# Covering a layer norm with matrix work: the order around it fixed, its chain put first, four more covering products; one pooled block moved ahead of the attention

## The chip, the cores and the metric

The kernel runs on one core of a Trainium2 chip. TensorE (PE in the profile) multiplies matrices out of SBUF into eight PSUM banks; VectorE (DVE) and ScalarE (ACT) do the elementwise work; SyncE (SP) issues the loads and stores, one after the other from one queue. The metric is the device time of one execution in microseconds (us), the median of several runs. Each engine works its own instructions in a fixed order and waits for the others through semaphores.

## The reference, cut to what matters

One step of a decoder layer on 16 meta, 512 prompt and 8 sample tokens, all in float32:

```python
z = h @ w_in + b_in                         # 2048 -> q 1024 | k 256 | v 256 | pool input u 1024
attn = sink_attention(rope(q), rope(k), v)  # window of 128, 16 heads, a learned sink for each
pool = (causal means of u over 2/4/8/16 - u) @ w_pool * pool_scale
h1 = layer_norm(alpha * h + concat(attn, pool) @ w_o)
a = silu(h1 @ w_gate) * (h1 @ w_up)         # 2048 -> 5632
y = layer_norm(alpha * h1 + a @ w_down)     # 5632 -> 2048
```

The 520 tokens that go past the mixer are worked in two halves of 260 columns (half 0 and half 1).

## The kernel before, in words

**A precise product.** A float32 weight is split into a high part (ACT, a CAST to `fp32r`, `split`, L181) and the remainder (DVE, L182), and so are the activations. A block of 128x128 weights then takes three passes on PE (`products`, L188, L189 and L191): high by high, high by low, low by high. A plain float32 matmul needs no split; the profile shows it as two records.

**The order.** The program is written once and an automatic scheduler sets each engine's order from a simulated timeline and from priorities. `with step(engine)` ties it down: what that engine does within the step comes after what it did in the step before.

**Attention.** `block("q0")` to `block("q7")` make the eight query blocks and `block("u0")` to `block("u7")` the eight pooled blocks: 96 matmuls each into two banks tagged `mm`, which DVE then empties. For each head pair t come the scores (`sc`, L525), the softmax on DVE and ACT, the turn of the probabilities (`tp`, L569 to L576) and the values (`o`, L587). Query and pooled blocks stand between, to cover the softmax and the copies. `pool_group(0)` to `pool_group(3)` (`pm`) are the small maps of the pooled blocks. `smT`, `smp`, `smpt`, `smo` are the sample tokens' attention.

**The two layer norms after the output projection.** `out_proj(h)` makes half h, and `ln1(h)` normalises it. `ln1` is a generator: each `yield` lets the caller put other work in. It takes the mean by a float32 matmul with a matrix of ones (L851, `mean`), subtracts it on DVE (L865), squares on ACT (L867), sums the squares by 16 float32 matmuls (L861, `var`), makes the reciprocal root (L221 to L227) and scales (DVE L879, ACT L882). The first layer norm runs beside `out_proj(1)`. The second has no such neighbour.

**Seven products in place of eight.** The gate and up projections use Winograd's form of Strassen's scheme: for each pair of weight tiles (a `Set`; `g0`, `u0`, `g1`, `u1`, ... up to 44) seven half-size products P1 to P7 of 24 matmuls. P1 needs the normalised half 0 alone (`b11`), P2 as well (`b21`); the other five need half 1, P3 to P6 through the operands `t1` to `t4` made from both halves (DVE L898 to L906, `put` L844 and L845), P7 through `t3`. DVE forms the weights' sums and differences (L927).

**The cover.** While the second layer norm runs, PE makes P1 of the first ten sets (`NFILL`, `Set.fill`, L951) from unsplit float32 operands, eight float32 matmuls each; ACT copies each result to SBUF (L953). No step holds this part: the scheduler chose where `mean`, `var` and the fills stand. Weight loads go through a ring of five buffers (`NRAW`); a fill's buffer comes free when its matmuls are done.

Of the kernel before, what the change touches and what calls it, by code (L numbers as in the profile page):

```python
# [13 lines left out]
P = 128  # L14
# [22 lines left out]
WPRIO = 400  # L37
NFILL = 10
NF = 5
LP = 600  # L40
WK = 7
WA = 4
# [21 lines left out]
def hybrid_step(ctx, tc, xin, w_in, w_o, w_g, w_u, w_d, w_pool, par_d, cst_d, ident_d, ln2gb, kct_d, vc_d, hist_d,  # L64
                ck_d, cv_d, sp_d, yp, ys, nkp, nvp, npp, nks, nvs, nps):
    nc = tc.nc
# [173 lines left out]
    with ExitStack() as sa:  # L240
# [183 lines left out]
        for h in range(2):  # L424
            for g in range(4):
                n = h * 4 + g + 1
# [316 lines left out]

        sample = sample_attention()
        block("q0")
        order = ["q1 q2", "q3 u0", "q4 u1", "q5 u2", "q6 u3", "q7 u4", "u5 u6", "u7"]
        for t in range(8):
            with step(pe):
                if t:
                    att_values(t - 1)  # L750
                sc = att_scores(t, qs.pop(t))
                if t >= 6:
                    next(sample)
            att_softmax(t, sc)
            done, us = us, []
            if t == 7:
                with step(pe):
                    for u in done:
                        next(u)
                    next(pool_group(2))  # L760
            for n, name in enumerate(order[t].split()):
                if n == 1:
                    with step(pe):
                        att_turn(t)
                        for u in done:
                            next(u)
                        if t == 6:
                            next(sample)
                    if t in (3, 5):
                        with step(pe):  # L770
                            next(pool_group((t - 3) // 2))
                block(name)
        with step(pe):
            att_turn(7)
# [72 lines left out]
    def ln1(h, zs):  # L847
# [15 lines left out]
        for k2 in range(8):  # L863
            a = z1[h][k2]
            nc.vector.tensor_sub(a, a, both(mean))  # L865
            sqs.append(t_tile(f"sq{h}_{k2}"))
            nc.scalar.activation(sqs[k2], a, AF.Square)  # L867
            if k2:
                var(k2 - 1)
            if k2 % 2:  # L870
                yield
        var(7)
        with tc.high_priority(LP):
# [38 lines left out]
    class Set:  # L912


        def __init__(self, w, i, name):
            self.w, self.i, self.name = w, i, name
            self.raw, self.p1 = {}, None

        def q(self, r, c):
            if (r, c) not in self.raw:  # L920
# [23 lines left out]
                    hi, lo = bop[b][k // 2]  # L944
                    products([bk], wh[:, sl], wl[:, sl], [hi[:, k % 2, :]], [lo[:, k % 2, :]], k == 0 and first, k == 7, True)

        def fill(self, t):

            bk = bank(f"p1_{self.name}")
            for k in range(8):  # L950
                nc.tensor.matmul(bk, self.q(0, 0)[:, k * P:(k + 1) * P], z1[0][k // 2][:, k % 2, :], start=(k == 0),  # L951
                                 stop=(k == 7))
            nc.scalar.copy(t, bk)  # L953
            self.p1 = t
            self.raw = {}

        def run(self, c11, c12, c21, c22):

            r = row_tile(f"p_{self.name}")
            filled = self.p1 is not None  # L960
            al, ga, de = [bank(f"{n}_{self.name}") for n in ("pa", "pc", "pd")]
            if not filled:
                self.p1 = r[:, HALF[0]]
                self.prod(1, al)
                nc.scalar.copy(self.p1, al)
            self.prod(7, ga)
# [234 lines left out]
```

## Time and profile before

| | |
|---|---|
| median of 3 runs | 2011.4 us (2010.8 to 2012.12) |
| the profiled execution's own time | 2010.83 us |
| its span, first to last instruction | 2009.0 us |
| PE busy | 1964.4 us, 98% of the span |
| DVE busy | 1341.8 us, 67% |
| ACT busy | 903.6 us, 45% |
| mean granted clock of PE | 0.988 |

"Busy" counts a matmul from its start to its modelled end, so PE counts as busy while matmuls come one after the other, at whatever speed they come. The granted clock says at what share of full speed PE was let run. A row of the timeline gives start, length, engine, line, output and input, and in square brackets how long the engine stood idle before it and what it waited for.

### The profile page before, as it was taken

What the parts mean: (1) busy time and instruction counts of PE and PEld (TensorE: products, weight loads), DVE (VectorE), ACT (ScalarE), POOL (GpSimd) and SP (SyncE); (2) the same over time, 40 slices, a digit from 0 to 9 for tenths busy, and PEclk for the clock granted to TensorE, in tenths of its full rate; (3) what the DMA queues carried; (4) which work ended last, traced back from release to release, by engine and by line L of the source; (5) the groups of instructions that cost most, each with busy time, mean ns of one, the idle gap of its engine ahead of it and who ended that gap; (6) DMA issues with size and microseconds to landing.
All of it is one profiled execution on the core that took longest, in us unless ns stands there. A gap on an engine that the chain in (4) does not pass through costs nothing.

```text
span 2009.0 us, 39879 instructions
## 1 busy us (share of the span) xinstructions
PE 1964.4 (98%) x16083; PEld 1936.3 (96%) x16083; DVE 1341.8 (67%) x2458; ACT 903.6 (45%) x1757; POOL 2.5 (0%) x8
## 2 busy tenths in 40 slices
PE   8999999999998999999999999999999999999996
PEld 8989999999978999999999999999999999999996
DVE  6666666766758888778777877787773433333586
ACT  6643445544554444544554455445552322222442
POOL 0000000000000000000000000000000000000000
PEclk9999999999998999999999999999999999999998
DMA  8622222665743444333333333333374633323554
GB/s 264 225 84 72 71 87 70 210 200 169 237 152 106 153 142 146 107 125 118 124 109 122 121 121 112 119 123 120 114 249 125 186 124 90 116 91 98 164 178 138
DMA packets 105625, 275.48 MB, mean 137 GB/s; under 512 B 12176, under 2 KB 35288, under 8 KB 105336
## 3 DMA queue, kind: packets, MB, share of 16 engines
q1 hardware_dynamic: 104320, 270.83, 42.2%
q8 instruction: 126, 2.06, 0.4%
q10 hardware_dynamic: 1120, 2.10, 0.3%
q14 instruction: 59, 0.48, 0.1%
HBM read 248.02 MB, written 27.41 MB: 137 GB/s over the span
## 4 chain that ended last, share of the span: by engine, by line
PE 94%; DVE 3%; DMA 1%; ACT 1%; issue 0%; SPq 0%; DVEq 0%; ACTq 0%
PE d L191 6%; PE d L189 6%; PE d L188 6%; PE pa_g L188 4%; PE pa_u L188 4%; PE pa_u L191 4%; PE pa_g L189 4%; PE pa_u L189 4%; PE pa_g L191 4%; PE o L188 3%; PE o L191 3%; PE o L189 3%; PE pc_g L188 2%; PE pc_u L188 2%; PE pc_g L189 2%; PE pc_u L191 2%
## 5 line engine op out<-in xcount | busy, mean ns | idle before, releaser
L181 ACT CAST rr<-fr 128x512 fp32r<-128x512 f32 (+1 forms) x1064 | 644.3, 612 | 918.4 <-PE d L189 245.1
L182 DVE TENSOR_TENSOR rr<-fr,rr 128x512 fp32r<-128x512 f32 (+1 forms) x1064 | 703.0, 677 | 414.7 <-ACT rr L181 401.0
L927 DVE TENSOR_TENSOR fr<-fr 128x1024 f32<-128x1024 f32 x176 | 215.3, 1223 | 64.0 <-DMA fr<-in_w_g_dram 32.2
L188 PE MATMUL d<-rr 128*128 128x260 f32 x736 | 191.4, 281 | 0.0
L189 PE MATMUL d<-rr 128*128 128x260 f32 x672 | 175.5, 283 | 0.0
L191 PE MATMUL d<-rr 128*128 128x260 f32 x736 | 148.2, 282 | 0.0
L188 PE MATMUL o<-rr 128*128 128x260 f32 x512 | 146.1, 286 | 0.3 <-ACT rr L181 0.3
L191 PE MATMUL o<-rr 128*128 128x260 f32 x512 | 144.4, 283 | 0.2 <-DVE rr L182 0.2
L189 PE MATMUL o<-rr 128*128 128x260 f32 x512 | 144.3, 282 | 0.0
L188 PEld LDWEIGHTS d<-rr 128*128 128x128 f32 x736 | 138.5, 188 | 0.0
L188 PE MATMUL pa_g<-rr 128*128 128x260 f32 x454 | 129.1, 284 | 3.8 <-ACT rr L844 2.9
L191 PE MATMUL pa_g<-rr 128*128 128x260 f32 x454 | 128.8, 284 | 0.0
L188 PE MATMUL pa_u<-rr 128*128 128x260 f32 x454 | 128.6, 283 | 0.0
L191 PE MATMUL pa_u<-rr 128*128 128x260 f32 x454 | 128.0, 282 | 0.0
L189 PEld LDWEIGHTS d<-rr 128*128 128x128 f32 x672 | 126.3, 188 | 0.0
L189 PE MATMUL pa_g<-rr 128*128 128x260 f32 x420 | 119.4, 284 | 1.9 <-DVE rr L845 1.9
L189 PE MATMUL pa_u<-rr 128*128 128x260 f32 x420 | 118.6, 282 | 0.0
L191 PEld LDWEIGHTS d<-rr 128*128 128x128 f32 x736 | 113.2, 188 | 0.0
L188 PE MATMUL pc_g<-rr 128*128 128x260 f32 x352 | 101.7, 289 | 1.7 <-ACT rr L844 1.7
L189 PE MATMUL pc_g<-rr 128*128 128x260 f32 x352 | 101.1, 287 | 0.2 <-DVE rr L845 0.2
L191 PE MATMUL pc_g<-rr 128*128 128x260 f32 x352 | 100.6, 286 | 0.0
L188 PE MATMUL pc_u<-rr 128*128 128x260 f32 x352 | 99.9, 284 | 0.0
(417 smaller groups left out, 5459.1 us busy)
## 6 DMA issues: line engine op xcount, KB each, us to landing
fr<-in_w_g_dram SPq DMA_DIRECT2D x93, 512.0 KB, 4.4
fr<-in_w_u_dram SPq DMA_DIRECT2D x93, 512.0 KB, 4.5
fr<-in_w_d_dram SPq DMA_DIRECT2D x80, 512.0 KB, 3.6
fr<-in_w_o_dram SPq DMA_DIRECT2D x64, 512.0 KB, 4.5
fr<-in_w_in_dram SPq DMA_DIRECT2D x46, 512.0 KB, 4.1
fr<-in_w_d_dram SPq DMA_DIRECT2D x80, 192.0 KB, 2.4
a_d<-fr SPq DMA_DIRECT2D x44, 260.0 KB, 2.0
fr<-a_d SPq DMA_DIRECT2D x44, 260.0 KB, 3.6
```

The source lines that it names most:

```text
L181: nc.scalar.copy(wh, s)
L182: (lo or nc.vector).tensor_sub(wl, s, wh.bitcast(F32))
L188: nc.tensor.matmul(o, wh, hi[j], start=first, stop=False, skip_group_check=onto)
L189: nc.tensor.matmul(o, wh, lo[j], start=False, stop=False, skip_group_check=onto)
L191: nc.tensor.matmul(o, wl, hi[j], start=False, stop=last, skip_group_check=onto)
L927: op(self.q(*t), self.q(*a), self.q(*b))
```

## The change

**At the second layer norm.** `fill` becomes `ahead(n, t)`, a generator that makes P1 (n=1) or P2 (n=2) from float32 operands. The first two sets (`NKEEP = 2`: `g0` and `u0`) get both P1 and P2 and leave them in their four PSUM banks until `run` takes them up; the next ten get P1, copied to SBUF as before. That is 14 covering products of eight float32 matmuls, and 4 x 24 matmuls fewer in the products after. `ln1(1)` no longer yields between its squares. PE's order is fixed by steps: half of the first product, the mean, the other half, all 16 matmuls of the variance, then the 13 products. The chain of the layer norm is handed to the scheduler with a high priority.

**In the attention.** `block("u0")` is done right after `block("q0")`, ahead of the first scores; the other pooled blocks move up by one place, so that one stands alone in the turns 6 and 7, and `pool_group(2)` moves from turn 7 to turn 6.

```diff
+NKEEP = 2
...
         block("q0")
-        order = ["q1 q2", "q3 u0", "q4 u1", "q5 u2", "q6 u3", "q7 u4", "u5 u6", "u7"]
+        block("u0")
+        order = ["q1 q2", "q3 u1", "q4 u2", "q5 u3", "q6 u4", "q7 u5", "u6", "u7"]
...
             att_softmax(t, sc)
             done, us = us, []
-            if t == 7:
+            names = order[t].split()
+            block(names[0])
+            with step(pe):
+                if t < 7:
+                    att_turn(t)
+                for u in done:
+                    next(u)
+                if t == 6:
+                    next(sample)
+            if t in (3, 5, 6):
                 with step(pe):
-                    for u in done:
-                        next(u)
-                    next(pool_group(2))
-            for n, name in enumerate(order[t].split()):
-                if n == 1:
...
+                    next(pool_group((t - 2) // 2))
+            for name in names[1:]:
                 block(name)
...
-            if k2 % 2:
+            if k2 % 2 and h == 0:
                 yield
...
-        def fill(self, t):
-            bk = bank(f"p1_{self.name}")
+        def ahead(self, n, t=None):
+            self.bk[n] = bk = bank(f"p{n}_{self.name}")
             for k in range(8):
-                nc.tensor.matmul(bk, self.q(0, 0)[:, k * P:(k + 1) * P], z1[0][k // 2][:, k % 2, :], start=(k == 0),
-                                 stop=(k == 7))
-            nc.scalar.copy(t, bk)
-            self.p1 = t
+                nc.tensor.matmul(bk, self.q(0, n - 1)[:, k * P:(k + 1) * P], z1[0][4 * (n - 1) + k // 2][:, k % 2, :],
+                                 start=(k == 0), stop=(k == 7))
+                if k == 3:
+                    yield
+            if t is not None:
+                nc.scalar.copy(t, bk)
+                self.p1 = t
+                del self.bk[n]
             self.raw = {}
+            yield
 
         def run(self, c11, c12, c21, c22):
             r = row_tile(f"p_{self.name}")
             filled = self.p1 is not None
-            al, ga, de = [bank(f"{n}_{self.name}") for n in ("pa", "pc", "pd")]
+            al, de = [self.bk.get(n) for n in (1, 2)]
             if not filled:
                 self.p1 = r[:, HALF[0]]
-                self.prod(1, al)
+                if al is None:
+                    al = bank(f"p1_{self.name}")
+                    self.prod(1, al)
                 nc.scalar.copy(self.p1, al)
...
-            self.prod(2, de)
+            if de is None:
+                de = bank(f"p2_{self.name}")
+                self.prod(2, de)
...
     g1 = ln1(1, zs1)
-    for j, s in enumerate(sets[:NFILL]):
+    fills = [s.ahead(n) for n in (1, 2) for s in sets[:NKEEP]]
+    for j, s in enumerate(sets[NKEEP:NKEEP + NFILL]):
         if j % 2 == 0:
             f = pb.tile([P, 2, HN], F32, tag="fill", name=f"fill{j}", bufs=NF)
-        for _ in range(2):
+        fills.append(s.ahead(1, f[:, j % 2, :]))
+    pe = nc.tensor
+    for f in (fills[0], g1, fills[0], g1):
+        with step(pe):
+            next(f)
+    for j, f in enumerate(fills[1:]):
+        with tc.high_priority(LP if j < 9 else 0):
             next(g1, None)
-        s.fill(f[:, j % 2, :])
+        with step(pe):
+            for _ in f:
+                pass
```

The lines after the first are one further down in the changed kernel, so that the three passes stand there at L189, L190 and L192.

**PE's order at the second layer norm.** Before, from the mean on, with the row that follows the last fill (`p1_` is a fill's bank; `pc`, `pa` and `pd` are the banks of P7, P6 and P2; `x8` is eight instructions in a row):

```order
L851 MATMUL mean1_5996<-fr_60 128x260
L861 MATMUL var1_5999<-fr_60 128x260 x2
L951 MATMUL p1_g0_6006<-fr_60 128x260 x8
L951 MATMUL p1_u0_6033<-fr_60 128x260
L861 MATMUL var1_5999<-fr_60 128x260 x6
L951 MATMUL p1_u0_6033<-fr_60 128x260 x7
L861 MATMUL var1_5999<-fr_60 128x260 x6
L951 MATMUL p1_g1_6061<-fr_60 128x260 x7
L861 MATMUL var1_5999<-fr_60 128x260 x2
...
L951 MATMUL p1_u4_6226<-fr_60 128x260 x8
L188 MATMUL pc_g0_6238<-rr_61 128x260
```

Now, the same stretch:

```order
L951 MATMUL p1_g0_5996<-fr_60 128x260 x4
L850 MATMUL mean1_6002<-fr_60 128x260
L951 MATMUL p1_g0_5996<-fr_60 128x260 x4
L860 MATMUL var1_6009<-fr_60 128x260 x16
L951 MATMUL p1_u0_6057<-fr_60 128x260 x8
L951 MATMUL p2_g0_6073<-fr_60 128x260 x8
L951 MATMUL p2_u0_6091<-fr_60 128x260 x8
L951 MATMUL p1_g1_6109<-fr_60 128x260 x8
...
L951 MATMUL p1_u5_6266<-fr_60 128x260 x8
L189 MATMUL p7_g0_6278<-rr_61 128x260
```

The mean has half a product ahead of it and half behind it, the 16 variance matmuls stand together where before they were spread over three fills, and 13 products follow. After them come 24 matmuls of P7 in a row, where before the first 93 rows went to and fro between P7, P2 and P6.

**SP's queue at the end of the fills.** Before, from the last store of the normalised half 1 (L884) to the loads of the set `u0` (L1077 loads the constants of the last layer norm):

```order
L884 DMA h1_d_65<-fr_60 128x2x260
L173 DMA fr_60<-in_w_g_dram 128x1024 x2
L173 DMA fr_60<-in_w_u_dram 128x1024 x2
L1077 DMA fr_60<-in_ln2gb_dram 128x512 x3
L173 DMA fr_60<-in_w_u_dram 128x1024 x2
```

Now, with four loads for fills after that store, then the four loads of `g0` and those of `u0` (the constants are L1098):

```order
L883 DMA h1_d_65<-fr_60 128x2x260
L174 DMA fr_60<-in_w_g_dram 128x1024
L174 DMA fr_60<-in_w_u_dram 128x1024
L174 DMA fr_60<-in_w_g_dram 128x1024
L174 DMA fr_60<-in_w_u_dram 128x1024
L174 DMA fr_60<-in_w_g_dram 128x1024
L1098 DMA fr_60<-in_ln2gb_dram 128x512 x2
L174 DMA fr_60<-in_w_g_dram 128x1024
L1098 DMA fr_60<-in_ln2gb_dram 128x512
L174 DMA fr_60<-in_w_g_dram 128x1024 x2
```

Three loads of constants that stood within the loads of `u0` now stand between the first and the third load of `g0`.

**PE's order at the first scores.** Before, from the end of `q0`'s block (`tpv` are transposes of the values, `sc0` the scores of head pair 0, each followed by more of its kind):

```order
L191 MATMUL mm_q0_1_949<-rr_61 128x260
L472 MATMUL tpk1_911<-fr_60,mid_a_62 128x128
L473 MATMUL tpk1_911<-fr_60,mid_a_62 8x128
L482 MATMUL tpv0_917<-fr_60,mid_a_62 128x128 x4
L482 MATMUL tpv1_929<-fr_60,mid_a_62 128x128 x4
L525 MATMUL sc0_0_0_1064<-mid_a_62 128x152
```

Now:

```order
L192 MATMUL mm_q0_1_949<-rr_61 128x260
L473 MATMUL tpk1_911<-fr_60,mid_a_62 128x128
L474 MATMUL tpk1_911<-fr_60,mid_a_62 8x128
L189 MATMUL mm_u0_0_1065<-rr_61 128x276
...
L483 MATMUL tpv0_917<-fr_60,mid_a_62 128x128 x4
L189 MATMUL mm_u0_1_1066<-rr_61 128x260
...
L192 MATMUL mm_u0_1_1066<-rr_61 128x260
L526 MATMUL sc0_0_0_1184<-mid_a_62 128x152
```

The 96 matmuls of `u0` stand between `q0` and the scores, with the transposes of the values among them.

More of the change, by code (lines that the diff above doesn't have):

```diff
@@ L755, in hybrid_step @@
             done, us = us, []
-            if t == 7:
-                with step(pe):
-                    for u in done:
-                        next(u)
-                    next(pool_group(2))
-            for n, name in enumerate(order[t].split()):
-                if n == 1:
[L763 to L771, printed above, removed]
+            names = order[t].split()
[8 more added lines that the diff above has]
+            if t in (3, 5, 6):
+                with step(pe):
+                    next(pool_group((t - 2) // 2))
+            for name in names[1:]:
                 block(name)
@@ L916, in __init__ @@
             self.w, self.i, self.name = w, i, name
-            self.raw, self.p1 = {}, None
+            self.raw, self.bk, self.p1 = {}, {}, None
         def q(self, r, c):
@@ L960, in run @@
             filled = self.p1 is not None
-            al, ga, de = [bank(f"{n}_{self.name}") for n in ("pa", "pc", "pd")]
+            al, de = [self.bk.get(n) for n in (1, 2)]
             if not filled:
                 self.p1 = r[:, HALF[0]]
-                self.prod(1, al)
+                if al is None:
+                    al = bank(f"p1_{self.name}")
+                    self.prod(1, al)
                 nc.scalar.copy(self.p1, al)
+            else:
+                al = bank(f"p1_{self.name}")
+            ga = bank(f"p7_{self.name}")
             self.prod(7, ga)
```

## The prediction

> **What bounds the kernel now.** First the page: busy time, and the chain that ended last.
>
> ```profile
> PE 1964.4 (98%) x16083; PEld 1936.3 (96%) x16083; DVE 1341.8 (67%) x2458; ACT 903.6 (45%) x1757; POOL 2.5 (0%) x8
> PE 94%; DVE 3%; DMA 1%; ACT 1%; issue 0%; SPq 0%; DVEq 0%; ACTq 0%
> ```
>
> PE sets the end. A change pays only where PE waits or runs slowly, or where it gets less to do. Next the windows by stage (PE, PEld, DVE, ACT, POOL, granted clock, DMA share, GB/s):
>
> ```profile
> 552.00:597.70 45.70, 42.84 (x195) 36.67 (x194) 24.91 (x40) 22.60 (x46) 0.00 (x0) 1.00 0.49 156
> 597.70:626.80 29.10, 20.22 (x96) 17.27 (x94) 25.78 (x41) 14.62 (x24) 0.00 (x0) 0.71 0.27 82
> 660.00:1330.00 670.00, 670.00 (x5587) 669.85 (x5586) 528.85 (x779) 329.04 (x598) 0.00 (x0) 1.00 0.38 124
> ```
>
> The last row is the steady state: 5587 matmuls in 670.0 us, 0.120 us each and never idle, so nothing is to be had there. The row above it is the end of the second layer norm: 96 matmuls in 29.1 us, 0.30 us each, at a clock of 0.71. PE's timeline shows this hole from the output projection's last matmul:
>
> ```profile
> 551.88 0.28 PE L191 MATMUL o<-rr 128*128 128x260 f32 x1
> 553.15 0.71 PE L851 MATMUL mean<-fr 128*128 128x260 f32 x2 [0.98 <-DVE fr L835]
> 555.72 1.15 PE L861 MATMUL var<-fr 128*128 128x260 f32 x4 [1.87 <-ACT fr L867]
> ...
> 576.89 3.67 PE L951 MATMUL p_g<-fr 128*128 128x260 f32 x16
> 580.40 3.67 PE L951 MATMUL p_u<-fr 128*128 128x260 f32 x16
> ...
> 597.74 0.47 PE L188 MATMUL pc_g<-rr 128*128 128x260 f32 x1
> 600.30 0.39 PE L188 MATMUL pc_g<-rr 128*128 128x260 f32 x1 [1.48 <-ACT rr L844]
> 604.01 0.42 PE L189 MATMUL pd_g<-mid_b,rr 128*128 128x260 f32 x1
> 604.23 0.42 PE L191 MATMUL pd_g<-mid_b,rr 128*128 128x260 f32 x1
> 618.23 0.59 PE L188 MATMUL pa_g<-rr 128*128 128x260 f32 x1 [2.89 <-ACT rr L844]
> 626.79 0.28 PE L191 MATMUL pa_g<-mid_b,rr 128*128 128x260 f32 x1
> ```
>
> PE waits for the mean, then for the squares; once the fills are used up at 597.74, it waits for the operands t1 to t4 (ACT L844), and while it waits the granted clock falls: at 604.01 a matmul comes 0.22 us after the one before, where 0.12 is usual. Only at 626.79 does the steady pace begin.
>
> **The layer norm, part by part.**
>
> *What the hole costs.* The next matmul could have come at 552.00. The mean comes at 553.15: 1.15 lost. Its float32 matmul takes an eighth of a fill, (580.40 - 576.89)/8 = 0.44, so the variance could start at 553.59; it starts at 555.72: 2.13 lost. From 597.74 to 626.79 stand 94 of the window's 96 matmuls (the others start just ahead of it and at its end). At 0.120 they take 11.3 of 29.05: 17.8 lost. Together 21.1 us.
>
> *What is added.* A covering product takes 3.51 us; the 24 matmuls that it replaces take 24 x 0.120 = 2.88. Ten products were there before; four more cost 4 x 0.63 = 2.5 us. By the Trainium skill (FP8 and Floating Point Precision, TensorE Precision Notes) a true float32 matmul is four passes through the array. From that, as an estimate, a product would be 32 x 0.120 = 3.84 us, the four 3.8 us instead of 2.5 and the forecast 1.3 us higher; the trace has 3.51, which decides.
>
> *What is still waited for.* Half a product (1.75) now covers the wait for the mean (1.15). From the mean's start to the variance's first matmul the trace has 2.57; the mean (0.44) and the other half (1.75) fill all but 0.4. The 16 variance matmuls run behind each other, 7.0 us, since a pair takes 0.88 and a square comes sooner (ACT's second row: four in 2.56). ACT's and DVE's timeline:
>
> ```profile
> 553.89 0.38 ACT L853 COPY fr<-mean 128x260 f32<-128x260 f32 x1 [8.37 <-PE mean L851]
> 555.03 2.56 ACT L867 ACTIVATE fr<-fr 128x520 f32<-128x520 f32 x4 [0.77 <-DVE fr L865]
> 573.22 0.43 DVE L221 TENSOR_SCALAR fr<-var 128x260 f32<-128x260 f32 x1 [13.95 <-PE var L861]
> 577.86 4.97 DVE L879 TENSOR_TENSOR fr<-fr 128x520 f32<-128x520 f32 x8
> 583.97 0.69 DVE L899 TENSOR_TENSOR fr<-fr 128x520 f32<-128x520 f32 x1
> 584.58 0.69 DVE L845 TENSOR_TENSOR rr<-fr,rr 128x520 fp32r<-128x520 f32 x1
> 619.88 1.48 DVE L845 TENSOR_TENSOR rr<-fr,rr 128x520 fp32r<-128x520 f32 x2
> ```
>
> The variance now ends at 552.0 + 1.75 + 0.44 + 1.75 + 0.4 + 7.0 = 563.4, against 573.2 before, and the 13 other products end at 563.4 + 45.6 = 609.0.
>
> *Is the chain done by then?* From the variance's end to the first scaling it is 4.6 us (573.22 to 577.86), then 5.0 for eight scalings, then on DVE 16 subtractions and 20 remainders at 0.61 (583.97 to 584.58): 22.0. That ends at 595.0, if DVE never waits. ACT's copies of the fills stand among its casts, and PE's products pace them: the last casts stand behind the copy of the tenth product, which ends at 609.0 - 4 x 3.51 = 595.0, so some 597. Twelve us to spare; without them the 13 products would be too few, and PE would wait as now. Before, the chain needed until 621.36 (the last row), since it began 10 us later and shared DVE with the first weights' differences.
>
> *Are the weights there?* A buffer comes free when a fill's matmuls end, so the second load of g0 goes out with the end of the eleventh product, at 598.5. Two loads of constants stand ahead of it in SP's queue; they may go once the chain has left its scratch tiles (597). SP's queue, the loads' landing between 535 and 640 us, and what DVE and ACT make of them:
>
> ```profile
> 591.12 3.85 SPq L173 DMA_DIRECT2D fr<-in_w_g_dram  x2
> 598.13 13.93 SPq L173 DMA_DIRECT2D fr<-in_w_u_dram  x2
> 620.60 1.59 SPq L1077 DMA_DIRECT2D fr<-in_ln2gb_dram  x3
> fr<-in_w_g_dram SPq DMA_DIRECT2D x12, 512.0 KB, 5.9
> 593.67 1.22 DVE L927 TENSOR_TENSOR fr<-fr 128x1024 f32<-128x1024 f32 x1 [1.84 <-DMA fr<-in_w_g_dram]
> 594.93 1.14 ACT L181 CAST rr<-fr 128x512 fp32r<-128x512 f32 x2 [3.02 <-DVE fr L927]
> ```
>
> Landing 5.9 (the median between 535 and 640 us), the difference 1.2, a cast 0.6 and a remainder 0.7 make 598.5 + 8.4 = 606.9: 2 us ahead of PE. The bounds of a wait here are 0 and some 4.5 us (the constants first, their landing and the load's in a row); I take 0, nearest to the sum of the rows. This is the thinnest margin of the whole forecast.
>
> *Net:* 21.1 - 2.5 - 0.4 = **18.2 us** gained. The copies of P1 and P7 that the two kept sets put on ACT stand beside five products (14.4 us of PE), with ACT idle half the time.
>
> **The attention's start.** PE's and DVE's timeline:
>
> ```profile
> 99.73 1.37 PE L482 MATMUL tpv<-fr,mid_a 128*128 128x128 f32 x8
> 104.04 3.42 PE L525 MATMUL sc<-mid_a 64*128 64x152 f32 x16 [2.94 <-DVE mid_a L381]
> 107.39 0.40 PE L188 MATMUL mm_q<-rr 128*128 128x276 f32 x1
> 329.26 1.82 PE L525 MATMUL sc<-mid_a 64*128 64x152 f32 x16
> 99.59 0.90 DVE L506 TENSOR_SCALAR fr<-mm_q,fr 128x276 f32<-128x276 f32 x2 [1.97 <-PE mm_q L191]
> 103.17 0.72 DVE L381 TENSOR_TENSOR mid_a<-fr 128x536 f32<-128x536 f32 x1
> ```
>
> The first scores wait for q0's rotation (L381), and then run at half speed: 3.42 us, where sc7 takes 1.82. From the first transpose to q1 it is 107.39 - 99.73 = 7.66 us; at full speed the eight transposes take 0.9 (twelve take 1.47 in a row below) and the scores 1.8, so 5.0 are lost. With u0 there, 96 x 0.12 = 12 us of matmuls cover the rotation. u0's first bank is q0's, and PE waits until DVE has read it, half of its first row later (99.59 + 0.45 = 100.04, against q0's end at about 99.6): 0.4. Bounds: 0 (u0 held by its own weights as long as the scores were) to 5.0; I take 5.0 - 0.4 = **4.6**, since q1, in the place that u0's splits now take, started without a wait of its own.
>
> **The attention's end.** In turn 7 the softmax, two pooled chains and u7's splits met on DVE and ACT:
>
> ```profile
> 341.13 0.39 PE L191 MATMUL mm_u<-rr 128*128 128x276 f32 x1 [0.88 <-DVE rr L182]
> 312.41 1.47 PE L576 MATMUL tp<-fr,mid_a 128*128 128x128 f32 x12
> 313.15 1.52 ACT L577 COPY mid_a<-tp 128x512 f32<-128x512 f32 x3
> ```
>
> Now u7's four splits stand ahead of sc7's softmax, so the 0.88 goes. In turn 6, pool_group(2) (24 x 0.12 = 2.9 us) covers alone what u6's 12 us covered: ACT's copies of the turned probabilities, which end 0.8 us after the transposes (314.67 against 313.88). Bounds: +1.2 (that wait, and what u7 had to spare behind it) and -3 (the values wait in turn 6, as the first scores did for their 2.94); I take **1.0**.
>
> **Sum.** 18.2 + 4.6 + 1.0 = 23.8 us. The profiled execution took 2010.83, so 1987.0; the median of the runs is 0.6 above it. I say 1987.
>
> **The rivals.**
>
> *A. The weights come late* (place: P7 of g0). If the constants go ahead and land first, PE waits 4.5 us; the clock then falls as it did in the window 597.70:626.80, a slow stretch of 604's kind, some 3 us more. 1994.5. For it: three loads moved into g0's own. Against: the chain that holds them ends 12 us earlier than the fills.
>
> *B. The clock falls anyway.* By the Trainium skill (TensorE: Matmul & The Clock Gate, "Why this matters for your kernels") the clock drops after PE has been idle for more than about 3 us. The trace has half-speed matmuls at 604 with no wait over 1.9 us ahead of them. If the waits did not cause the slow clock and it returns, the part stays that slow matmuls cost: in 597.70:626.80 the clock of 0.71 means 0.58 of the 29.1 us at half speed, so with the 96 matmuls spread evenly 56 that took 0.10 too long. 6 us: 1993. Against it: the steady row, 670 us at 1.00 without a wait; I hold the waits for the cause.
>
> *C. The attention loses what it gains.* Turn 6 waits 3 us and scores at half speed follow, 1.6, as at the first scores: the attention nets 4.6 + 1.0 - 4.6 = 1.0, the sum 19.2. 1992. For it: 2.9 us of cover in the place of 12. Against: the copies need 0.8 of them.
>
> *D. The constants block the queue: slower than before.* SP issues in order, and L1077 went out at 620.60 only, when the chain was through. Now loads of g0 stand behind it. If the chain again takes the 43.5 us from its first scaling to its last remainder (577.86 to 621.36), it ends at 568.0 + 43.5 = 611.5, P7 starts 12 us late, and a slow stretch (B's 6 us) comes on top: 2005. It gets slower than before from the point where the constants go out after 618: one microsecond of issues and 8.4 for load and split start P7 at 627.4, 18.4 late, and with B's 6 the 23.8 are gone. At 622 it would be 2015. For it: ACT's casts of the chain wait among the copies of the fills, and DVE for the casts. Against: no weight difference stands before the chain's last remainder on DVE now.
>
> *E. No effect:* the wait for t1 to t4 only moves behind the longer row of fills. 2011. For it: nothing on DVE or ACT gets less. Against: the chain would have to end 18 us after the fills, against 12 us before them in the sum.
>
> **How the numbers follow.** The plan as summed 0.73 (1983 to 1991); A 0.10; B 0.04; C 0.07; E 0.03; D 0.03. A measurement of this kernel tells a difference from about 0.2%, 4 us: the first four are faster, E the same, D slower. The range takes in A, B and C, and goes 4 us below the sum: 0.4 and 0.2 from the attention's bounds, and two more scores or values freed of half speed (1.6 each, as the first scores). 1983 to 1995.
>
> **What would show it.** Right: between the output projection's last matmul and P7 no wait over 0.6 us; the variance done about 11.5 us after that matmul, P7 about 57 us after it, followed by 0.12 us a matmul at clock 1.00; no wait of `sc` for L381. Wrong: a `p7_g` or `mm_u` row with a wait on a DMA, L182 or L843; an `o` row that waits for ACT in turn 6; the constants issued later than the fills' end.

## The result, and the profile after

The changed kernel takes 1992.5 us (median of four, 1990.0 to 1997.1) against 2011.8 before (four, 2010.8 to 2012.5): a ratio of 0.9907, 95% interval 0.9888 to 0.9926, so 15 to 22 us faster. The forecast was 1987.0 within 1983 to 1995; 19.3 of the 23.8 us came. The profiled execution is the longest of the four (1997.12 us); another profiled execution of the same kernel, from the experiments, took 1991.29.

The page after, busy time and the chain that ended last:

```profile
PE 1960.8 (98%) x16051; PEld 1932.7 (97%) x16051; DVE 1336.8 (67%) x2450; ACT 898.1 (45%) x1749; POOL 2.5 (0%) x8
PE 94%; DVE 2%; DMA 2%; ACT 1%; issue 0%; SPq 0%; DVEq 0%; ACTq 0%
```

PE is the bound as before. Windows by stage of the kernel after (PE, PEld, DVE, ACT, POOL, granted clock, DMA share, GB/s): the covering products, the first weight sets, the steady state.

```profile
550.00:607.00 57.00, 56.88 (x262) 48.98 (x260) 40.90 (x65) 29.82 (x59) 0.00 (x0) 1.00 0.56 176
607.00:640.00 33.00, 29.60 (x229) 28.79 (x228) 23.99 (x35) 15.74 (x30) 0.00 (x0) 0.95 0.42 136
640.00:1325.00 685.00, 684.18 (x5706) 683.98 (x5705) 545.62 (x806) 335.66 (x607) 0.00 (x0) 1.00 0.38 125
```

The first row has no hole left. The second has a new one: 229 matmuls at 0.120 are 27.5 us and took 33.0. PE's timeline of the kernel after, from the output projection's last matmul:

```profile
550.03 0.28 PE L192 MATMUL o<-rr 128*128 128x260 f32 x1
550.15 1.92 PE L951 MATMUL p_g<-fr 128*128 128x260 f32 x8
551.90 0.60 PE L850 MATMUL mean<-fr 128*128 128x260 f32 x2
552.34 1.91 PE L951 MATMUL p_g<-fr 128*128 128x260 f32 x8
554.37 7.31 PE L860 MATMUL var<-fr 128*128 128x260 f32 x32
561.51 3.67 PE L951 MATMUL p_u<-fr 128*128 128x260 f32 x16
...
603.59 3.67 PE L951 MATMUL p_u<-fr 128*128 128x260 f32 x16
606.91 0.47 PE L189 MATMUL p_g<-rr 128*128 128x260 f32 x1
...
617.27 0.58 PE L192 MATMUL p_g<-rr 128*128 128x260 f32 x1 [2.36 <-DVE rr L183]
617.65 0.42 PE L189 MATMUL p_g<-rr 128*128 128x260 f32 x1
617.87 0.42 PE L190 MATMUL p_g<-rr 128*128 128x260 f32 x1
```

The mean, the variance and P7 (606.91) come without a wait. Ten us behind P7 a product of g0 waits 2.36 us for a remainder, and then matmuls come 0.22 apart for a while. DVE and SP of the kernel after say what it waits for:

```profile
594.45 1.48 DVE L844 TENSOR_TENSOR rr<-fr,rr 128x520 fp32r<-128x520 f32 x2
...
609.72 1.22 DVE L926 TENSOR_TENSOR fr<-fr 128x1024 f32<-128x1024 f32 x1
...
615.39 1.23 DVE L926 TENSOR_TENSOR fr<-fr 128x1024 f32<-128x1024 f32 x1 [2.23 <-DMA fr<-in_w_u_dram]
616.53 1.89 DVE L183 TENSOR_TENSOR rr<-fr,rr 128x512 fp32r<-128x512 f32 x3
```

```profile
595.17 1.11 SPq L1098 DMA_DIRECT2D fr<-in_ln2gb_dram  x2
596.77 0.33 SPq L174 DMA_DIRECT2D fr<-in_w_g_dram  x1
597.15 0.42 SPq L1098 DMA_DIRECT2D fr<-in_ln2gb_dram  x1
600.28 3.83 SPq L174 DMA_DIRECT2D fr<-in_w_g_dram  x2
607.29 10.28 SPq L174 DMA_DIRECT2D fr<-in_w_u_dram  x4
```

The chain ended at 595.9, the constants were out by 597.6. But of the four loads of u0 the first left only at 607.29, with the last covering product, and the second at 611.00, when g0's last difference (609.72, 1.22 us long) had freed a buffer of the ring of five. The last row of SP's queue joins the four; a narrower window shows the second by itself, and SP's waits from 600 to 625 show what held it:

```profile
611.00 0.33 SPq L174 DMA_DIRECT2D fr<-in_w_u_dram  x1
SPq L174 <- DVE fr L926: 3.3, 1, 3.3
```

It landed at 615.29. u0's first difference (L926), which needs two loads, started at 615.39 on DVE, and g0's remainder (L183) stood behind it.

In the attention no score waits for the rotation any more:

```profile
L526 PE MATMUL sc<-mid_a x128: 289/375/394, 113.4 to 329.7; 64*128 64x256 f32 x96, 64*128 64x152 f32 x32
```

(128 of them, never an idle engine before one; before, one wait of 2.94.) At its end, though, windows of the kernel after and of its second trace, after_again (columns as above), differ:

```profile
306.00:310.00 4.00, 4.00 (x22) 4.00 (x22) 3.12 (x13) 3.96 (x17) 0.00 (x0) 0.57 0.66 212
347.00:358.00 11.00, 11.00 (x57) 8.60 (x57) 9.96 (x33) 7.55 (x21) 0.00 (x0) 0.53 0.68 211
```

```profile
305.00:312.00 7.00, 7.00 (x34) 7.00 (x34) 4.80 (x20) 4.51 (x20) 0.00 (x0) 0.51 0.48 150
343.00:352.00 9.00, 9.00 (x126) 7.44 (x125) 9.00 (x35) 5.48 (x15) 0.00 (x0) 1.00 0.58 180
```

Behind the decode samples' second small matmuls (smo, which start at 344.2 and 345.1) the same instructions run at half clock for 10.2 us in one execution, and not at all in the other.

**All traces by stage.** Times are differences of start times on PE: A, the attention, from q0's first matmul to the first variance matmul of the first layer norm; then from there to P7 of g0; then from P7 to the first matmul of the down projection's last part (d_0h). "Half" is the time at half clock behind smT and behind smo, in us. Each kernel is told of below.

| trace | A | half, smT / smo | var to P7 | P7 to d_0h |
|---|---|---|---|---|
| before | 375.96 | 3.4 / 3.4 | 134.46 | 1255.19 |
| after | 373.24 | 3.4 / 10.2 | 145.48 | 1232.37 |
| after_again | 370.32 | 6.8 / 0 | 145.47 | 1230.12 |
| norm_only | 375.94 | 3.4 / 3.4 | 145.47 | 1231.77 |
| attention_only | 371.90 | 6.8 / 3.4 | 134.44 | 1256.10 |
| tail_apart | 370.01 | 6.8 / 0 | 145.49 | 1229.49 |
| keep_g0_raw | 371.84 | 6.8 / 3.4 | 145.48 | 1230.01 |
| dve_order | 371.93 | 6.8 / 3.4 | 145.48 | 1228.95 |
| fills_12 | 371.92 | 6.8 / 3.4 | 138.47 | 1233.95 |
| samples_spread | 372.70 | 0 / 3.4 | 145.48 | 1230.79 |
| keep_one | 370.32 | 3.4 / 3.4 | 138.47 | 1233.56 |
| fills_10 | 371.88 | 6.8 / 3.4 | 131.45 | 1250.73 |
| keys_spread | 368.04 | 0 / 3.4 | 145.47 | 1229.93 |
| twelve_and_order | 367.63 | 0 / 3.4 | 138.45 | 1235.65 |

### The profile page after: what moved, and what is told of

Read it like the earlier page. It is cut to its first block, busy times and chain, and to the rows that moved or that the text cites. A ratio compares the mean times of both kernels' runs of the same rounds, so it can differ in the third digit from the quotient of the medians.

```text
span 1995.3 us, 39815 instructions
## 1 busy us (share of the span) xinstructions
PE 1960.8 (98%) x16051; PEld 1932.7 (97%) x16051; DVE 1336.8 (67%) x2450; ACT 898.1 (45%) x1749; POOL 2.5 (0%) x8
## 4 chain that ended last, share of the span: by engine, by line
PE 94%; DVE 2%; DMA 2%; ACT 1%; issue 0%; SPq 0%; DVEq 0%; ACTq 0%
PE p_u L189 7%; PE p_u L192 7%; PE p_u L190 7%; PE p_g L192 7%; PE p_g L189 7%; PE p_g L190 7%; PE d L192 6%; PE d L190 6%; PE d L189 6%; PE o L189 3%; PE o L192 3%; PE o L190 3%; PE mm_q L189 2%; PE mm_u L189 2%; PE mm_u L192 2%; PE mm_u L190 2%
## 5 line engine op out<-in xcount | busy, mean ns | idle before, releaser
L183 DVE TENSOR_TENSOR rr<-fr,rr 128x512 fp32r<-128x512 f32 (+1 forms) x1056 | 698.2, 677 | 411.3 <-ACT rr L182 399.1
L926 DVE TENSOR_TENSOR fr<-fr 128x1024 f32<-128x1024 f32 x176 | 215.3, 1224 | 71.2 <-DMA fr<-in_w_g_dram 39.0
L192 PE MATMUL p_g<-rr 128*128 128x260 f32 x800 | 226.5, 283 | 2.4 <-DVE rr L183 2.4
L189 PE MATMUL p_u<-rr 128*128 128x260 f32 x800 | 226.8, 284 | 1.3 <-DVE fr L991 1.3
L189 PE MATMUL p_g<-rr 128*128 128x260 f32 x800 | 227.2, 284 | 0.5 <-DVE fr L991 0.5
L192 PE MATMUL p_u<-rr 128*128 128x260 f32 x800 | 225.5, 282 | 0.0
L190 PE MATMUL p_g<-rr 128*128 128x260 f32 x768 | 217.3, 283 | 0.0
L190 PE MATMUL p_u<-rr 128*128 128x260 f32 x768 | 216.9, 282 | 0.0
L189 PE MATMUL d<-rr 128*128 128x260 f32 x736 | 191.4, 281 | 0.0
L190 PE MATMUL d<-rr 128*128 128x260 f32 x672 | 175.5, 283 | 0.0
L192 PEld LDWEIGHTS p_g<-rr 128*128 128x128 f32 x800 | 151.6, 189 | 2.7 <-DVE rr L183 2.7
L189 PEld LDWEIGHTS p_u<-rr 128*128 128x128 f32 x800 | 150.6, 188 | 1.8 <-DVE fr L991 1.8
L189 PEld LDWEIGHTS p_g<-rr 128*128 128x128 f32 x800 | 151.1, 189 | 0.8 <-DVE fr L991 0.7
L192 PEld LDWEIGHTS p_u<-rr 128*128 128x128 f32 x800 | 151.1, 189 | 0.0
L192 PE MATMUL d<-rr 128*128 128x260 f32 x736 | 148.2, 282 | 0.0
L189 PE MATMUL o<-rr 128*128 128x260 f32 x512 | 146.7, 287 | 0.3 <-ACT rr L182 0.3
L190 PEld LDWEIGHTS p_g<-rr 128*128 128x128 f32 x768 | 144.9, 189 | 0.0
L192 PE MATMUL o<-rr 128*128 128x260 f32 x512 | 144.4, 284 | 0.2 <-DVE rr L183 0.2
L190 PE MATMUL o<-rr 128*128 128x260 f32 x512 | 144.6, 283 | 0.0
L190 PEld LDWEIGHTS p_u<-rr 128*128 128x128 f32 x768 | 144.5, 188 | 0.0
L189 PEld LDWEIGHTS d<-rr 128*128 128x128 f32 x736 | 138.5, 188 | 0.0
```

What stands on the lines that cost most here:

```text
L183: (lo or nc.vector).tensor_sub(wl, s, wh.bitcast(F32))
L189: nc.tensor.matmul(o, wh, hi[j], start=first, stop=False, skip_group_check=onto)
L190: nc.tensor.matmul(o, wh, lo[j], start=False, stop=False, skip_group_check=onto)
L192: nc.tensor.matmul(o, wl, hi[j], start=False, stop=last, skip_group_check=onto)
L926: op(self.q(*t), self.q(*a), self.q(*b))
```

## The experiments

Eleven further kernels and the changed one again, in three groups of four; each group has its own runs of the kernel before beside it (2011.9, 2011.5 and 2012.2 us).

### The two parts apart, and the same kernel again

norm_only has the attention's blocks and turns as before (the first diff, against the changed kernel; the loop over the turns goes back with it); attention_only has the layer norm, the sets and the ten fills as before (the second diff; all edits of `ln1`, `Set` and the list of fills go back). after_again is the changed kernel unaltered.

```
-        block("u0")
-        order = ["q1 q2", "q3 u1", "q4 u2", "q5 u3", "q6 u4", "q7 u5", "u6", "u7"]
+        order = ["q1 q2", "q3 u0", "q4 u1", "q5 u2", "q6 u3", "q7 u4", "u5 u6", "u7"]
...
```

```
-NKEEP = 2
...
-        def ahead(self, n, t=None):
+        def fill(self, t):
...
```

> The layer norm's part of the change alone; the attention has the order of the kernel before. Theory 1 (the traced losses are the change's own: 5.5 us in the first two weight sets, where u0's weights come late): the norm part gives about 12 us, so 2000 us against 2011.8, and in the trace a third product of g0 waits over 2 us for DVE's remainder again. Rival (the forecast's 18.2 was right and the profiled execution of the changed kernel was an unlucky one): 1993.5 us, and no matmul of the first two sets waits more than 0.6 us.

> The attention's part alone; the layer norm as before. Theory 1 (6.8 us gained up to the decode samples' last matmuls, 4 given back behind them at half speed and with two kinds of matmul mixed): 2.0 to 2.8 us faster than before, 2009.4 us, with a half-speed stretch of about 10 us around 347 in the trace. Rival (the forecast's 5.6): 2006.2 us, with a half-speed stretch of 3.4 us there, as before.

> The changed kernel once more, unaltered, for a second trace and a time beside the others. Theory 1: 1992 us, and both losses are in the second trace too (a wait over 2 us in g0's third product, a half-speed stretch of 10 us behind the decode samples). Rival (chance): the second trace lacks at least one of them, and an execution without either takes 1988.

norm_only: 1997.2 us, ratio 0.9926 (0.9914 to 0.9939): 14.6 us of gain. Its waits on PE behind the output projection:

```profile
PE p_g L192 <- DVE rr L183: 1.9, 1, 1.9
PE p_g L189 <- DVE fr L993: 0.5, 1, 0.5
PE p_u L189 <- DVE fr L993: 0.5, 1, 0.5
```

The wait for the remainder is there without any change in the attention, so it belongs to the new row of products; 14.6 lies between the two theories' 12 and 18.2. attention_only: 2007.9 us, ratio 0.9979 (0.9971 to 0.9988), 3.9 us of gain, also between; its trace has 3.4 us at half clock behind smo, as the rival said, but 6.8 behind smT. The two add up to 18.5, nearly the 19 of the whole: within what the runs tell apart, the gains of the parts add. after_again: 1992.9 us, ratio 0.9906. Its trace has the wait (1.8 us) but no half clock behind smo, and that profiled execution took 1991.3 us, 5.8 less than the first. So the wait came in both traces of this kernel (and in norm_only, tail_apart, keys_spread and samples_spread, 1.7 to 1.9 us), the long stretch at half clock in one.

### The attention's end

tail_apart gives the values of turn 7 a step of their own:

```
         for p in range(2):
+            if p == 0:
+                with step(pe):
+                    att_values(7)
+                    next(sample)
             with step(pe):
                 next(g3)
                 next(us[0])
-                if p == 0:
-                    att_values(7)
-                    next(sample)
```

> The changed kernel, but in the attention's end the values of turn 7 have a step of their own ahead of the last pooled block, so that PE runs o 32 times in a row and the 12 pm matmuls behind them, as the kernel before did, in place of pm, o, pm, o, pm, o. Theory 1 (the mixing of the two costs the 2.7 us between the samples' end and the output projection, and keeps the clock down for two further stretches of 3.4 us): 3 to 4 us faster than the changed kernel, 1988.5 us, the half-speed stretch 3.4 us long. Rival (the clock falls behind the samples' 64 small matmuls and stays down by chance, whatever the order): 1992 us, within 1 us of the changed kernel.

1992.1 us, ratio 0.9905 (0.9890 to 0.9920), against 1992.9 for the changed kernel beside it: no difference that can be told. PE's timeline of the second trace of the changed kernel, and then of tail_apart:

```profile
347.97 2.39 PE L588 MATMUL o<-mid_a 16*64 16x128 f32 x26
350.29 0.51 PE L189 MATMUL pm<-rr 128*128 128x260 f32 x2
350.73 0.43 PE L588 MATMUL o<-mid_a 128*64 128x128 f32 x2
```

```profile
345.84 2.82 PE L588 MATMUL o<-mid_a 16*64 16x128 f32 x32
```

The order became what was meant. Both traces have no half clock behind smo, and between them A differs by 0.3 us only (370.32 and 370.01). At equal clock the mixing is worth 0.3 us, not 3; theory 1 on the tail falls. What costs there is the clock, and the next two runs ask where it comes from. In keys_spread a generator emits the 32 smT (32 records in the trace, 16 float32 matmuls in the program) in portions of eight from within u6, one behind each quarter; in samples_spread a second one (`values`, the same way) also emits the 64 smo behind u7's last four quarters:

```
                 mm(ws[-1], 2 * h + g, js[:1] if apart else js)
+                next(side[0], None)
...
+            def keys():
                 for b in range(NS):
...
+                    if b % 2:
+                        yield
+            side[0] = keys()
```

> The changed kernel, but the decode samples' small matmuls (32 smT in 3.8 us, 64 smo in 2.0 us) run in four portions each between quarters of u6's matmuls and between the last quarters of u7's, in place of one stretch. Theory 2 (the clock is halved after a 3.4 us period in which PE streams little, however busy it reads; a stretch of small matmuls makes such a period, and where the period falls decides by chance): no half-speed stretch near 306 and 347, 3 to 4 us faster than the changed kernel, 1989 us. Rival (the clock falls there for another reason, such as waits or the transfers): the stretches stay, 1992 us.

> The changed kernel, but only the samples' first small matmuls (smT) are spread over the quarters of u6's; the second (smo) stay in their place, so that the wait of 3.1 us for their bank that the run with both spread had brought does not come. Theory 2 (a 3.4 us period of little streaming halves the clock for the next): no half-speed stretch near 306; 3.4 us faster than the changed kernel, 1989 us. Rival: a half-speed stretch behind the scores nonetheless, 1992 us.

samples_spread: 1993.6 us, ratio 0.9906 (0.9892 to 0.9921), not faster. In its trace the half clock behind smT is gone, but the edit brought a wait of its own, and with it the clock fell (from 344.73 on):

```profile
344.94 0.39 PE L640 MATMUL tpu<-fr,mid_a 128*15 128x128 f32 x1 [3.15 <-DVE fr L746]
```

keys_spread leaves smo alone: 1990.1 us, ratio 0.9885 (0.9869 to 0.9902), and its A is 368.04. The window of smT in one piece in the kernel after, and then windows of keys_spread:

```profile
302.88:306.30 3.42, 3.42 (x33) 3.42 (x31) 3.42 (x20) 1.64 (x8) 0.00 (x0) 1.00 0.17 41
```

```profile
306.00:320.00 14.00, 14.00 (x121) 13.98 (x120) 8.79 (x29) 7.44 (x25) 0.00 (x0) 1.00 0.33 100
347.00:351.00 4.00, 4.00 (x31) 3.11 (x28) 3.19 (x12) 3.27 (x9) 0.00 (x0) 0.60 0.96 257
```

The portions of smT start at 305.93, 309.76, 313.60 and 317.47, and the clock is 1.00 through all of them; behind smo, still in one piece, it falls as before. In the eleven traces with smT in one piece there is a stretch of 3.4 or 6.8 us at half clock behind it, eleven times of eleven, with no wait of PE ahead of it; in the three with smT spread there is none. So a stretch of small matmuls halves the clock although PE reads busy (all of the 3.42 us from 302.88 on, after which the clock falls at 306.43), as theory 2 says. On the time alone the run is inconclusive: its interval overlaps the changed kernel's.

### Behind P7

keep_g0_raw (first diff) puts g0's two covering products last and keeps their weights; dve_order (second) ties u0's first product behind g0's last on DVE:

```
-    fills = [s.ahead(n) for n in (1, 2) for s in sets[:NKEEP]]
+    fills = [sets[1].ahead(n) for n in (1, 2)]
...
+    fills += [sets[0].ahead(n) for n in (1, 2)]
...
+            if self.name != "g0":
                 self.raw = {}
```

```
+            with step(*[nc.vector] * (self.name == "u0")):
                 self.prod(7, ga)
...
+            with step(*[nc.vector] * (self.name == "g0")):
                 self.prod(3, al, False)
```

> g0's two covering products stand last in the row, and the weights they use stay in their two buffers for g0's own products, so that g0 loads two tiles instead of four and u0's first load goes out with the end of the twelfth covering product instead of the fourteenth. Theory 1 (u0's loads go out too late, and that costs the 1.8 to 2.4 us wait for DVE's remainder and the later ones for L991): no wait over 0.6 us in the first two sets, 3.5 us faster than the changed kernel, 1989 us. Rival (DVE's order alone is to blame): the wait stays, as u0's difference still stands ahead of g0's remainder, 1992 us.

> The changed kernel, but on DVE u0's first difference and its remainders stand behind those of g0's last product; loads and buffers as they were. Theory 1 (loads): g0's product no longer waits, but u0's P7 does, for its own weights: their landing is 615.4, and with difference 1.2, cast 0.6 and remainder 0.7 they are ready at 618, 3 us before g0 would end at 621 without a wait; so by these rows the wait of 1.8 to 2.4 us goes and is not replaced: 1990 us. Rival (the later loads hang on the same buffers): the wait comes back further on, at P6 or P5 of u0, and the time stays at 1992 us.

keep_g0_raw: 1991.1 us, ratio 0.9893 (0.9877 to 0.9910); dve_order: 1990.4, 0.9889 (0.9875 to 0.9904). Neither differs from the changed kernel by more than the runs can tell. PE's waits behind P7 in keep_g0_raw, and in dve_order:

```profile
615.61 0.39 PE L189 MATMUL p_g<-rr 128*128 128x260 f32 x1 [0.52 <-DVE fr L992]
623.32 0.39 PE L192 MATMUL p_u<-rr 128*128 128x260 f32 x1 [1.47 <-DVE rr L183]
```

```profile
617.33 0.39 PE L189 MATMUL p_g<-rr 128*128 128x260 f32 x1 [1.40 <-DVE fr L992]
```

In keep_g0_raw the wait moved from g0 to u0; in dve_order it moved to the row that empties a bank (L992). From P7 to d_0h they save 0.1 and 1.2 us against after_again. But neither edit removed what it was meant to remove. In keep_g0_raw u0's first load left 7 us earlier than in after_again (596.59 and 603.74), the second only 2.3 (604.90 and 607.21), again when g0's last difference had freed a buffer, and u0's first difference on DVE began no earlier. Its row in after_again, and in keep_g0_raw:

```profile
611.08 1.23 DVE L926 TENSOR_TENSOR fr<-fr 128x1024 f32<-128x1024 f32 x1 [1.72 <-DMA fr<-in_w_u_dram]
```

```profile
611.22 1.23 DVE L926 TENSOR_TENSOR fr<-fr 128x1024 f32<-128x1024 f32 x1 [1.85 <-DMA fr<-in_w_u_dram]
```

So theory 1, that u0's loads go out too late, was hardly put to the test; what the run speaks against is that the one load which waits for the last covering product costs it. The rival there had the wait stay in g0, and it did not. In dve_order u0's first difference still stands on DVE ahead of the row that PE waits for:

```profile
615.72 1.22 DVE L926 TENSOR_TENSOR fr<-fr 128x1024 f32<-128x1024 f32 x1
616.86 0.42 DVE L992 TENSOR_TENSOR fr<-fr,p_g 128x260 f32<-128x260 f32 x1
```

Its rival is right in that a wait comes back and little is gained; the place that it named, P6 or P5 of u0, is not where the longest one came. In all three traces a wait of 1.4 to 1.8 us comes somewhere in the first two sets.

### How many covering products

fills_12, fills_10 and keep_one each alter one constant, in this order:

```
-NFILL = 10
+NFILL = 8
```

```
-NFILL = 10
+NFILL = 6
```

```
-NKEEP = 2
+NKEEP = 1
```

> Twelve covering products instead of fourteen. Price theory (each costs 0.63 us more than the matmuls it replaces, and there were 12 us to spare): P7 starts 7 us earlier, with no wait as long as the weights keep pace, and the kernel is 1.3 us faster, 1991 us. Rival (the chain's last casts stand behind a covering product's copy and the loads behind the chain, so that two fewer leave the weights late): PE waits 3 to 5 us at P7 of g0, 1994 us or more.

> Ten covering products, as many as the kernel before had, with everything else of the change. Theory (the chain ends 45.8 us after the output projection's last matmul and ten products end 42.7 us after it, by the rows; the weights' loads stand behind the chain): PE waits 4 to 10 us at P7 of g0 and in it, part of it at half speed, and the gain over twelve is turned into a loss: 1993 to 1998 us. Rival (the earlier start of the variance and the priority do all the work and the four further products are only cover for cover): P7 starts at once, 1.3 us faster than with twelve, 1987.5 us.

> Only g0 keeps two products in banks; ten sets are filled, so twelve covering products again, as many as in the run with twelve, but u0 has seven products of its own but one instead of five. Theory 3 (a set that keeps two products has 14.4 us of matmuls instead of 20.2 for the same four loads and four differences, and its P5 follows P6 into the same bank, so that PE waits 0.5 us for the bank: the kept sets are what is short): one kept set fewer takes away 1 us or more of the waits behind P7, 1 us faster than the run with twelve, 1987.7 us. Rival (only the number of covering products counts): the same as the run with twelve, 1988.8 us, with the same sum of waits (1.7 us) behind P7.

fills_12: 1988.8 us, ratio 0.9883 (0.9869 to 0.9898). fills_10: 1998.2 us, 0.9929 (0.9915 to 0.9943), at the upper end of its theory. keep_one: 1986.9 us, 0.9872 (0.9855 to 0.9888). PE's waits in fills_10 behind the output projection, and its DVE:

```profile
PE p_g L192 <- DVE rr L183: 2.9, 1, 2.9
PE p_g L190 <- DVE rr L844: 1.6, 1, 1.6
PE p_g L189 <- ACT rr L843: 1.3, 2, 1.1
```

```profile
592.28 2.34 DVE L926 TENSOR_TENSOR fr<-fr 128x1024 f32<-128x1024 f32 x2
594.55 0.69 DVE L897 TENSOR_TENSOR fr<-fr 128x520 f32<-128x520 f32 x1
...
603.65 1.47 DVE L844 TENSOR_TENSOR rr<-fr,rr 128x520 fp32r<-128x520 f32 x2
```

With ten products PE catches up with the chain and waits for its operands (L843, L844), as before the change. The weights' differences (L926) again stand among the chain's rows on DVE, and its last remainder comes 54.5 us after the variance's start (605.1; 41.6 in the kernel after, 595.9). The price of a product follows from the table: fills_12 to after_again is 7.00 us more ahead of P7 for two products, and 48 matmuls, 5.76 us, fewer behind it: 0.62 each, as summed (0.63). Against the matmuls that are left (before: 1255.19 less the 17.8 of the hole, 1237.4; less 0.120 for each one replaced), the part behind P7 loses 13.3 us with ten, 2.0 to 4.1 with twelve (three traces) and 3.1 to 6.5 with fourteen (eight). From the variance to d_0h all three traces with twelve (1372.0 to 1374.1) are shorter than all eight with fourteen (1374.4 to 1377.9). The price explains 1.2 us of it; why the first sets lose less behind twelve was not tested.

keep_one has the rival's time: from the variance to d_0h it is 0.4 us shorter than fills_12 (1372.03 and 1372.42), and the waits are 2.0 us against 1.7. All are in g0 now, the kept set, and u0 has none, which is what theory 3 says of the place; of the size it was wrong. Over fills_12 it gains nothing that the runs can tell.

### The version that the runs point to

twelve_and_order is fills_12, keys_spread and tail_apart in one.

> Three edits together, as the version that the runs point to: twelve covering products, the samples' first matmuls spread over u6's quarters, and the values of turn 7 ahead of the last pooled block. If their gains add (3.5, 3.4 and 0.8 us against the changed kernel): 1985 us. Rival (stretches at half speed only move elsewhere): 1988 us.

1985.6 us (1983.4 to 1986.7), ratio 0.9866 (0.9850 to 0.9881): faster than both kernels, about 7 us below the changed one, whose interval (0.9888 to 0.9926) it does not touch. A is the shortest of all (367.63). The part behind P7 lost more than in fills_12 (1235.65 against 1233.95), most of it in one wait of 1.27 us at 1183. Its interval overlaps those of fills_12 and keep_one, so what the two edits of the attention add to twelve products is told by A alone (367.63 against 371.92).

## Why the prediction was right, and where it was off

**The sign and the mechanism** held. The variance ended 11.4 us after the output projection's last matmul (forecast 11.4), P7 started 56.8 after it (57.0), the chain ended 11 us ahead of P7 (12) without a weight's difference in it, and the constants went out ahead of the covering products' end: rivals D and E are out. The residual wait ahead of the variance was 0.3 (0.4), the price of a product 0.62 (0.63). Additional products are needed, as fills_10 shows: without the four, 13.3 us are lost behind P7. But two of the four are enough (fills_12).

The number was less good than the range makes it look. 1992.5 lies outside the 1983 to 1991 of the plan as summed, to which 0.73 was given; the range holds it because it takes in the rivals. That rivals B (1993) and C (1992) name nearly this time is coincidence: the turns wait for nothing, and B's slow matmuls were put into the layer norm, where after_again has no half clock at all.

**The norm term** was 18.2 and came to 14.1 in the second trace (134.46 + 1255.19 before, 145.47 + 1230.12 then), 11.8 in the first, and to 14.6 in the runs of norm_only. The step that failed is "Are the weights there? ... I take 0". It looked at the load for P7, which was indeed there, and not at the next ones: u0's second load has to wait until g0's last difference has freed a buffer, and u0's first difference, waiting for that load, stands on DVE ahead of a remainder of g0. Its upper bound of 4.5 us is about what was lost (4.2 in the second trace), though at another place than rival A put it: in the third to the fifth product of g0 and later. In the first trace 5.5 us were lost there, since the clock fell on top (617.65, 0.22 a matmul).

What the loss is made of is known in part. Of the waits, 0.52 us stands at P5 of each kept set, which follows P6 into the same bank: in both sets in after_again, in u0 not at all in keep_one, where u0 is not kept. The 1.8 us for the remainder of g0 come by the way just told. That the ring of five buffers is what is short, or that the kept sets are, since they have 14.4 us of matmuls for the four loads and differences that other sets have 17 to 20 for, both fit; no run had a larger ring, and in keep_one the total did not fall, so this stays open. Waits of 1.7 us and more in all come in the first two sets at every setting. A wait of 0.8 us at 1014 in the first trace of the changed kernel (0.7 at 1008 in the second), behind a late load of g, is unexplained too.

**The attention's 5.6** was right at equal clock. Before, and in after_again, 6.8 us behind smT and smo ran at half clock, and A is 375.96 and 370.32: 5.64 less. The terms came out as well: up to the first smT PE takes 7.1 us longer (214.7 against 207.6) with one pooled block more, and such a block runs for 11.8 us, so 4.7 were gained there (forecast 4.6) and 0.9 behind it (1.0). Each further stretch of 3.4 us costs 1.3 to 1.6 (371.9 with three, 373.24 with four), and most of the traces with the new attention and smT in one piece have three, as attention_only has: 5.64 - 1.58 = 4.1, and its runs gave 3.9. No turn waits, so rival C is out. The step that was wrong here is the sentence in rival B, "I hold the waits for the cause" of the slow clock: behind smT and smo it falls without a wait, and the end term (1.0) counted PE's work and waits there but no clock.

So of the 4.5 us that were missing, about 4 are the weights of the first sets and 1.6 one more stretch at half clock; together a little more than is missing, within what the runs tell apart.

## What to carry to other kernels

A product that covers a wait takes its matmuls from the stage behind, while that stage keeps its loads and its work on the other engines: check not only the first transfer behind the cover but the next few, and try fewer covering products than the sum allows. Where a stretch of very small matmuls stands in one piece, look at the granted clock behind it, and try to spread it among large ones: here that took the slow stretch away, but a wait that it brought cost as much in samples_spread. When an in-order queue makes an engine wait, moving one row usually moves the wait; see first whether the total changes.

## What the runs showed of the hardware that was not expected

The granted clock goes down for stretches of 3.41 us and multiples of it (3.4, 6.8, 10.2; the long one before was 13.7). 32 records of float32 matmuls with 8 columns (smT, 3.8 us) brought one about in 11 of 11 traces, 64 with 4 columns (smo, 2.0 us) in 11 of 13, though PE reads 100% busy. A stretch costs about 1.5 us, by A in the table.

The length differs between executions of one kernel (10.2 and 0 us behind smo), and the traces show in part what it depends on. Within each trace all changes of the clock lie whole multiples of 3.413 us apart: in the trace before the half clock starts at 103.90, 298.46, 353.07 and 602.25, which is 57, 16 and 73 steps. Reckoned on this raster, smT in one piece starts 3.2 to 3.3 us into a step in the four traces with 3.4 us at half clock behind it, and 0.4 to 1.1 us into one in the seven with 6.8. So in the four it lies almost wholly in one step, and in the seven it is divided between two; the kernel after and after_again, one program, are one of each. For smo, no half clock goes with a start 2.2 to 2.4 us into a step (after_again, tail_apart), and 3.4 us with 2.5 to 3.1 (seven traces) and 0.4 to 0.5 (before and norm_only); at 0.1 and 0.2 us one has 3.4 (keep_one) and one 10.2 (the kernel after), which the raster alone does not explain. Where an execution falls on the raster was not set by any edit.

The start varies as well: from the first key and value matmul to q0's first it is 66.1 to 68.7 us in these traces with the same instructions on PE, 2.6 us of the scatter between runs of one kernel.
